# Other cuts of the last two rows, and a piece summed by two engines, in a ReLU row sum

## Chip and metric

The kernel runs on one core of a Trainium2 chip. The metric is the device time of one execution in microseconds (us); less is better. VectorE (DVE in the profile) and ScalarE (ACT) compute, SyncE (SP) issues the transfers, and 16 DMA engines carry them out.

## What is computed

The input has 32 x 512 = 16384 rows of 1024 float32 numbers, 67 MB. Each row gives one number: the sum of its positive elements.

```python
def reference(x):                     # x: (32, 512, 1024) float32
    relu_x = np.maximum(x, 0)
    return np.sum(relu_x, axis=-1).astype(np.float32)
```

## The kernel before

The rows are spread over 128 partitions, 128 rows on each. They fall into three regions of 1, 111 and 16 rows per partition (REGIONS); in the last one a partition holds 16 rows that lie one behind another in memory. The input comes in seven chunks of 16 rows per partition (CHUNKS), into a buffer `buf` with room for three chunks, and then in a tail of 8, 4 and 2 rows (TAIL) and the last two rows, which are cut into pieces. All transfers are issued by SyncE on one queue, in the order in which they are written.

In the first six chunks ScalarE applies ReLU to several rows at once (L145), and VectorE adds up each row (L160, `tensor_reduce`). In the seventh chunk and in the tail, both engines do whole rows by turns, ReLU and sum in one instruction. `on_act` (L127) does it on ScalarE and `on_dve` (L130) on VectorE; each shows in the profile as two rows, the pass itself and a short read of its accumulator.

The change is in what follows. `flat` is the place of the last two rows in `buf`, 2048 columns in one line: columns 0 to 1023 are the one row, from D = 1024 on the other. The queue brings, in this order:

| transfer | columns in `flat` | count | semaphore |
|---|---|---|---|
| first (L112) | 0 to 911 (CUT = 912) | 912 | `s_in[-3]` |
| second (L112) | 1536 to 2047 | 512 | `s_in[-2]` |
| third (L112) | 1280 to 1535 (from HEAD = 256 on) | 256 | `s_in[-1]` |
| seam (L115) | 912 to 1279, into the tile `seam` | 368 | `s_seam`, 16 counts |

The seam spans the end of the one row (w = 112 columns) and the head of the other (256). In the tile `seam` it lies between accumulators: two columns ahead of it for the two halves of the first piece, two behind it for the second and the third piece. When everything is there, one pass of ScalarE over `seam[:, 0:k]` (k = 2 + w) adds the rest of the one row to its two partial sums, and one pass of VectorE over the remaining columns does so for the other row. The partial sums are of positive numbers, so ReLU leaves them as they are.

Before these closing sums, ScalarE does the left half of the first piece and then the second piece alone (L194, L195); VectorE does the right half of the first piece and then the third (L197, L198). Both closing sums wait for `s_seam` to reach 16 + 2: the seam's transfer, the second piece and the third (L199, L202). ScalarE also waits for the halves (`s_half`).

On SyncE, the store of the first region's results is issued early. The store of the middle region (L123) waits for the third piece's transfer, and the last store (L207) for both closing sums (`s_last`). The program ends when all stores have landed.

Of the kernel before, what the change touches and what calls it, by code (L numbers as in the profile page):

```python
# [3 lines left out]
P = 128  # L4
D = 1024
# [4 lines left out]
ACT_STEPS = [[16], [7, 9], [7, 9], [7, 9], [4, 5, 7], [3, 4, 5]]  # L10
DVE_STEPS = [[4, 5, 7], [7, 4, 5], [7, 4, 5], [7, 4, 5], [4, 5, 7], [3, 4, 5]]
TAIL = [8, 4, 2]
CUT = 912
HEAD = 256


def bass_relu_sum_kernel(
# [14 lines left out]
    fp32 = mybir.dt.float32  # L32
# [5 lines left out]
    J = B * S // P  # L38
# [11 lines left out]

    buf = nc.alloc_sbuf_tensor("buf", [P, NB, BIG, D], fp32)
    w = D - CUT
    seam = nc.alloc_sbuf_tensor("seam", [P, 2 + w + HEAD + 2], fp32)
    res = nc.alloc_sbuf_tensor("res", [P, J], fp32)
    turned = nc.alloc_sbuf_tensor("turned", [P, 32], fp32)

# [1 line left out]
    s_in = [nc.alloc_semaphore(f"s_in{i}") for i in range(n_in)]  # L58
# [5 lines left out]
    s_seam = nc.alloc_semaphore("s_seam")  # L64
    s_last = nc.alloc_semaphore("s_last")
# [4 lines left out]
    sp, act, dve = nc.sync, nc.scalar, nc.vector  # L70
# [36 lines left out]

    rows = xv[-1].rearrange("p j d -> p (j d)")[:, r * D : (r + 2) * D]
    flat = buf[:, tb, r : r + 2, :].rearrange("p j d -> p (j d)")
    first, second, third = [(0, CUT), (D + D // 2, 2 * D), (D + HEAD, D + D // 2)]  # L110
    for k, (lo, hi) in enumerate((first, second, third)):
        sp.dma_start(out=flat[:, lo:hi], in_=rows[:, lo:hi]).then_inc(  # L112
            s_in[NBIG + len(TAIL) + k], 16
        )
    sp.dma_start(out=seam[:, 2 : 2 + w + HEAD], in_=rows[:, CUT : D + HEAD]).then_inc(s_seam, 16)  # L115
    sp.wait_ge(s_turn, 1)
# [9 lines left out]
    def on_act(t, acc):  # L126
        return act.activation(t, t, AF.Relu, accum_out=acc)  # L127

    def on_dve(t, acc):
        return dve.tensor_scalar(  # L130
            out=t, in0=t, scalar1=0.0, scalar2=None, op0=ALU.max, op1=ALU.add, accum_out=acc
        )
# [4 lines left out]
    k = 0  # L137
# [49 lines left out]
    lo, hi = first  # L187
    act.wait_ge(s_in[-3], 16)
    dve.wait_ge(s_in[-3], 16)
    on_act(flat[:, lo : CUT // 2], seam[:, 0:1]).then_inc(s_half, 1)  # L190
    on_dve(flat[:, CUT // 2 : hi], seam[:, 1:2]).then_inc(s_half, 1)
    k = 2 + w
    lo, hi = second
    act.wait_ge(s_in[-2], 16)  # L194
    on_act(flat[:, lo:hi], seam[:, k + HEAD : k + HEAD + 1]).then_inc(s_seam, 1)  # L195
    lo, hi = third
    dve.wait_ge(s_in[-1], 16)  # L197
    on_dve(flat[:, lo:hi], seam[:, k + HEAD + 1 : k + HEAD + 2]).then_inc(s_seam, 1)  # L198
    act.wait_ge(s_seam, 16 + 2)  # L199
    act.wait_ge(s_half, 2)  # L200
    on_act(seam[:, 0:k], res[:, J - 2 : J - 1]).then_inc(s_last, 1)
    dve.wait_ge(s_seam, 16 + 2)  # L202
    on_dve(seam[:, k : k + HEAD + 2], res[:, J - 1 : J]).then_inc(s_last, 1)


    sp.wait_ge(s_last, 2)
# [31 lines left out]
```

## Time and profile before

| what | value |
|---|---|
| time, median of 3 runs | 160.80 us (160.78 to 161.15) |
| span of the profiled execution, first to last instruction | 159.4 us |
| last semaphore record of the profiled execution | 160.85 us |
| VectorE busy | 120.6 us (76%) |
| ScalarE busy | 101.5 us (64%) |
| input read | 67.11 MB, 421 GB/s over the span |
| VectorE `tensor_reduce` of rows (L160) | 99.4 us in 18 instructions |
| ScalarE ReLU of several rows (L145) | 80.4 us in 13 instructions |

Times in the profile count from the first instruction of the span. The span leaves out what lies around it; the profiled execution's last record is at 160.85 us, so 1.46 us lie behind the span. A row such as "157.01 0.42 DVE L130" gives the start, the length, the engine and the line of an instruction; in brackets stands how long the engine had been idle ahead of it, and what ended that. L127 and L130 are the lines of the two helpers, so different passes are told apart by their shape: 128x456 is 128 partitions with 456 columns each.

### The profile page before, as it was taken

The page shows a single profiled execution, that of the slowest core. Times are in us where ns is not written, and L with a number is a line of the kernel's source. Part 1 is how long each engine was busy: PE and PEld are TensorE (multiplying, and loading weights), DVE is VectorE, ACT ScalarE, POOL GpSimd, SP SyncE. Part 2 cuts the span into 40 slices and gives each one's busy share as a digit, 9 for nine tenths or more (in the row PEclk, how much of TensorE's full clock was granted, in tenths as well). Part 3 has the DMA queues.
Part 4 walks back from the last instruction along what each step waited for, and adds up shares of the span by engine and source line. Part 5 has one row for each costly group of instructions (what it writes and reads, how often), then busy time and mean ns, then how long its engine had stood idle before and what let it go on. Part 6 is the DMA issues. An engine that isn't in the chain of part 4 may idle for free.

```text
span 159.4 us, 150 instructions
## 1 busy us (share of the span) xinstructions
DVE 120.6 (76%) x59; ACT 101.5 (64%) x54; POOL 0.2 (0%) x4
## 2 busy tenths in 40 slices
DVE  0000000009999999999999999999999999898995
ACT  3000059980799708996099941999329980496975
POOL 0000000000000000000000000000000000000000
DMA  9997996996996997989979969969969979798994
GB/s 378 493 401 339 493 526 263 526 526 263 526 493 296 526 444 345 526 378 411 526 312 477 526 263 526 526 263 526 526 263 526 444 345 526 321 469 374 417 400 142
DMA packets 2457, 67.18 MB, mean 421 GB/s; under 512 B 536, under 2 KB 792, under 8 KB 1176
## 3 DMA queue, kind: packets, MB, share of 16 engines
q1 hardware_dynamic: 2456, 67.18, 98.1%
q14 instruction: 1, 0.01, 0.0%
HBM read 67.11 MB, written 0.07 MB: 421 GB/s over the span
## 4 chain that ended last, share of the span: by engine, by line
DVE 55%; DMA 34%; ACT 9%; SPq 2%; issue 0%
DVE res L160 54%; DMA buf<-in_x_dram 34%; ACT buf L145 9%; SPq L101 1%; SPq L112 1%; DVE buf L130 0%; DVE seam L130 0%; SPq L91 0%; DVE turned L169 0%
## 5 line engine op out<-in xcount | busy, mean ns | idle before, releaser
L160 DVE TENSOR_REDUCE res<-buf 128x4 f32<-128x4096 f32 (+3 forms) x18 | 99.4, 5596 | 35.5 <-ACT buf L145 35.5
L145 ACT ACTIVATE buf<-buf 128x7168 f32<-128x7168 f32 (+5 forms) x13 | 80.4, 6233 | 46.1 <-DMA buf<-in_x_dram 46.1
L127 ACT ACTIVATE buf<-buf 128x1024 f32<-128x1024 f32 (+2 forms) x19 | 19.0, 999 | 8.9 <-DMA buf<-in_x_dram 8.9
L130 DVE TENSOR_SCALAR_CACHE_REDUCE buf<-buf 128x1024 f32<-128x1024 f32 (+2 forms) x19 | 20.7, 1143 | 1.7 <-DMA buf<-in_x_dram 1.6
L127 ACT ACTIVATION_READ_ACCUMULATOR buf<-buf 128x1 f32 x19 | 3.6, 188 | 0.0
L145 ACT ACT_TABLE_LOAD x1 | 1.3, 1283 | 1.3 <-PEq L223 1.3
L130 DVE DVE_READ_ACCUMULATOR buf<-buf 128x1 f32 x19 | 1.6, 84 | 0.0
L130 DVE TENSOR_SCALAR_CACHE_REDUCE seam<-seam 128x258 f32<-128x258 f32 x1 | 0.4, 421 | 0.0
L127 ACT ACTIVATE seam<-seam 128x114 f32<-128x114 f32 x1 | 0.3, 300 | 0.1
L169 DVE STREAM_TRANSPOSE turned<-res 128x32 f32<-128x32 f32 x1 | 0.2, 211 | 0.0
L127 ACT ACTIVATION_READ_ACCUMULATOR seam<-seam 128x1 f32 x1 | 0.2, 186 | 0.0
L223 POOL MEMSET const-bfloat16-1.0<- 128x1 bf16 x1 | 0.1, 101 | 0.0
L223 POOL MEMSET const-uint8-127<- 128x1 uint8 x1 | 0.1, 101 | 0.0
L223 POOL MEMSET const-float32-0.0<- 128x1 f32 x1 | 0.1, 98 | 0.2 <-issue 0.2
L223 POOL MEMSET const-float32-1.0<- 128x1 f32 x1 | 0.1, 98 | 0.0
L130 DVE DVE_READ_ACCUMULATOR seam<-seam 128x1 f32 x1 | 0.1, 82 | 0.0
## 6 DMA issues: line engine op xcount, KB each, us to landing
buf<-in_x_dram SPq DMA_DIRECT2D x1, 7680.0 KB, 21.1
buf<-in_x_dram SPq DMA_DIRECT2D x1, 4096.0 KB, 25.3
buf<-in_x_dram SPq DMA_DIRECT2D x1, 2048.0 KB, 29.9
buf<-in_x_dram SPq DMA_DIRECT2D x1, 1024.0 KB, 31.9
buf<-in_x_dram SPq DMA_DIRECT2D x1, 512.0 KB, 3.3
buf<-in_x_dram SPq DMA_DIRECT2D x1, 456.0 KB, 32.5
buf<-in_x_dram SPq DMA_DIRECT2D x1, 256.0 KB, 32.7
seam<-in_x_dram SPq DMA_DIRECT2D x1, 184.0 KB, 32.6
```

The source lines that it names most:

```text
L101: sp.dma_start(out=buf[:, tb, r : r + n, :], in_=xv[-1][:, r : r + n, :]).then_inc(s_in[NBIG + i], 16)
L112: sp.dma_start(out=flat[:, lo:hi], in_=rows[:, lo:hi]).then_inc(s_in[NBIG + len(TAIL) + k], 16)
L127: return act.activation(t, t, AF.Relu, accum_out=acc)
L130: return dve.tensor_scalar(out=t, in0=t, scalar1=0.0, scalar2=None, op0=ALU.max, op1=ALU.add, accum_out=acc)
L145: act.activation(t, t, AF.Relu).then_inc(s_act, 1)
L160: dve.tensor_reduce(out=res[:, c * BIG + r : c * BIG + r + n], in_=buf[:, c % NB, r : r + n, :], axis=X, op=ALU.add,).then_inc(s_dve, 1)
L169: dve.transpose(out=turned[:, :], in_=res[:, 0:32]).then_inc(s_turn, 1)
L223: nc = _bacc.Bacc("TRN2", target_bir_lowering=False, num_devices=1)
```

## The change

Four constants give the cuts. The first piece has 928 columns, the second 624, the third 192 and the seam 304 (96 of the one row, 208 of the other). The order on the queue stays. The second piece is summed by both engines: the first 420 columns (SHARE) by ScalarE, the other 204 by VectorE, which does so ahead of the third piece. So VectorE waits for the second piece's transfer too, there are three accumulators behind the seam and not two, and the closing sums wait for 16 + 3 counts.

```diff
-CUT = 912
-HEAD = 256
+CUT = 928
+HEAD = 208
+MID = 400
+SHARE = 420
...
-    seam = nc.alloc_sbuf_tensor("seam", [P, 2 + w + HEAD + 2], fp32)
+    seam = nc.alloc_sbuf_tensor("seam", [P, 2 + w + HEAD + 3], fp32)
...
-    first, second, third = [(0, CUT), (D + D // 2, 2 * D), (D + HEAD, D + D // 2)]
+    first, second, third = [(0, CUT), (D + MID, 2 * D), (D + HEAD, D + MID)]
...
     lo, hi = second
     act.wait_ge(s_in[-2], 16)
-    on_act(flat[:, lo:hi], seam[:, k + HEAD : k + HEAD + 1]).then_inc(s_seam, 1)
+    on_act(flat[:, lo : lo + SHARE], seam[:, k + HEAD : k + HEAD + 1]).then_inc(s_seam, 1)
+    dve.wait_ge(s_in[-2], 16)
+    on_dve(flat[:, lo + SHARE : hi], seam[:, k + HEAD + 1 : k + HEAD + 2]).then_inc(s_seam, 1)
     lo, hi = third
     dve.wait_ge(s_in[-1], 16)
-    on_dve(flat[:, lo:hi], seam[:, k + HEAD + 1 : k + HEAD + 2]).then_inc(s_seam, 1)
-    act.wait_ge(s_seam, 16 + 2)
+    on_dve(flat[:, lo:hi], seam[:, k + HEAD + 2 : k + HEAD + 3]).then_inc(s_seam, 1)
+    act.wait_ge(s_seam, 16 + 3)
     act.wait_ge(s_half, 2)
     on_act(seam[:, 0:k], res[:, J - 2 : J - 1]).then_inc(s_last, 1)
-    dve.wait_ge(s_seam, 16 + 2)
-    on_dve(seam[:, k : k + HEAD + 2], res[:, J - 1 : J]).then_inc(s_last, 1)
+    dve.wait_ge(s_seam, 16 + 3)
+    on_dve(seam[:, k : k + HEAD + 3], res[:, J - 1 : J]).then_inc(s_last, 1)
```

## The prediction

> **What bounds the kernel now.** I read the page first, then the chain of waits from its end backwards, then the instructions of the last 3.5 us in order of time, then the groups with shapes kept apart, for prices. The edit touches nothing that is issued ahead of the last two rows of a partition (DMA issues from 123.39 us on), so only the end can move.
>
> ```profile
> span 159.4 us, 150 instructions
> ...
> q14 instruction: 1, 0.01, 0.0%
> ```
>
> ```profile
> 124.39 32.60 DMA buf<-in_x_dram
> 156.99 0.02 issue
> 157.01 0.44 DVE buf L130 x2
> 157.45 0.02 issue
> 157.47 0.43 DVE seam L130 x2
> ```
>
> The second fence is the end of the chain: start, length, what. The third piece lands at 156.99, VectorE sums it for 0.44, and then the closing sum of the seam tile takes 0.43. In the order of time:
>
> ```profile
> 155.96 0.58 ACT L127 ACTIVATE buf<-buf 128x456 f32<-128x456 f32 x1
> 155.98 0.62 DVE L130 TENSOR_SCALAR_CACHE_REDUCE buf<-buf 128x456 f32<-128x456 f32 x1
> 156.53 0.08 DVE L130 DVE_READ_ACCUMULATOR buf<-buf 128x1 f32 x1
> 156.65 0.63 ACT L127 ACTIVATE buf<-buf 128x512 f32<-128x512 f32 x1
> 157.01 0.42 DVE L130 TENSOR_SCALAR_CACHE_REDUCE buf<-buf 128x256 f32<-128x256 f32 x1 [0.40 <-DMA buf<-in_x_dram]
> ...
> 157.47 0.30 ACT L127 ACTIVATE seam<-seam 128x114 f32<-128x114 f32 x1
> 157.47 0.42 DVE L130 TENSOR_SCALAR_CACHE_REDUCE seam<-seam 128x258 f32<-128x258 f32 x1
> 157.68 0.19 ACT L127 ACTIVATION_READ_ACCUMULATOR seam<-seam 128x1 f32 x1
> 157.82 0.08 DVE L130 DVE_READ_ACCUMULATOR seam<-seam 128x1 f32 x1
> 157.93 0.34 SPq L207 DMA_DIRECT2D out_dram<-res  x1
> ```
>
> VectorE stands idle for 0.40 us ahead of the third piece, while ScalarE works on the second: that is the room the edit uses. The trace's semaphore records give landings closer than the fences: first piece 155.934, second 156.626, third 156.988, seam 157.438. The closing sums wait for three things: ScalarE's second piece (signalled 157.380), the seam's landing (157.438) and VectorE's third piece (157.451). The chain names the last, but the landing is only 13 ns ahead of it. So taking work off the engines alone buys 13 ns; what is to gain further lies in the transfers and in the closing sums themselves.
>
> ```profile
> L130 DVE TENSOR_SCALAR_CACHE_REDUCE buf<-buf 128x1024 f32<-128x1024 f32 x17 | 19.8, 1217 | 1.3 <-DMA buf<-in_x_dram 1.2
> ...
> L127 ACT ACTIVATE buf<-buf 128x512 f32<-128x512 f32 x1 | 0.6, 630 | 0.0
> L130 DVE TENSOR_SCALAR_CACHE_REDUCE buf<-buf 128x456 f32<-128x456 f32 x1 | 0.6, 624 | 0.0
> L127 ACT ACTIVATE buf<-buf 128x456 f32<-128x456 f32 x1 | 0.6, 584 | 0.0
> ```
>
> Prices from here (mean ns of one): a VectorE sum costs (1217 - 624) / 568 = 1.04 ns a column, a ScalarE sum (630 - 584) / 56 = 0.82 ns. Packets of the DMA records: 2048 bytes 84 ns, 1024 bytes 46 ns, so 0.037 ns a byte, and with 8 packets of a piece on each of the 16 engines 1.19 ns a column of a piece.
>
> **The change, part by part.**
>
> *Transfers.* The order on the queue and the total of 2048 columns stay, so the seam's landing stays at 157.438 by bytes alone. The first piece has 16 columns more (+19 ns: 155.953). After the second, 1552 columns are in instead of 1424 (+152 ns: 156.778). After the third, 1744 instead of 1680 (+76 ns: 157.064).
>
> *Where the pieces begin.* The second and the third now begin 5696 and 4928 bytes into the two rows, no longer at a multiple of 256 bytes. Before, only the seam does so (3648), and its 1472-byte packets take 66 ns in the median where the line through 1024 and 2048 bytes gives 62.6; so I price an odd start at 3.4 ns a packet, 27 ns a piece: second 156.805, third 157.118, seam 157.492. The bounds: nothing at all below; above, the slowest of those packets took 82 ns, 19 ns more than the line, 0.16 us a piece, 0.31 us for both.
>
> The Trainium skill speaks against this part (DMA: Bandwidth & Descriptors, "How a descriptor splits into AXI transactions"): a read that does not begin at a 256-byte boundary starts at the boundary below and pays for the unused bytes, in beats of 32. By that rule the two pieces would fetch 2 beats more per packet each and the seam, now 128 bytes above a boundary and not 64, 2 more as well; 6 beats times 8 packets at that page's 850 MHz would make an estimate of 0.06 us, where the row above makes 0.05. The trace's 66 against 62.6 ns agrees with it in sign. No sum below uses it.
>
> *The first piece's halves* grow from 456 to 464 columns: +8 ns on VectorE, +7 ns on ScalarE. ScalarE is done at 156.66 and VectorE at 156.62, both ahead of the second landing at 156.805, which hides it. Without that cover it would cost 8 ns.
>
> *The second piece* is split. Both engines start 0.024 us after it lands (156.988 to 157.012 in the third): 156.829. ScalarE's 512 columns took 0.732 us to their signal; 420 take 92 x 0.82 = 0.075 less: 157.486, later than the 157.380 of before, as the piece lands later. VectorE's new sum is 204 columns: 420 - 52 x 1.04 = 366 ns. The wait is one more in front of the third piece's sum, and behind it stand the third sum and VectorE's closing sum. Sums in a row start their own length less 73 ns apart (154.838 to 155.982 for 1217 ns, with a wait between), so VectorE is free for the third at 157.122. That lies in the idle 0.40 us. Its own transfer releases the third later, at 157.118 + 0.024 = 157.142: the new sum is hidden, by 20 ns. If that cover were gone, each ns would go onto the end.
>
> *The third piece* has 192 columns: 0.439 - 64 x 1.04 ns = 0.372 us to its signal, so 157.514. That is the last of the three, with the seam at 157.492. The closing sums start 23 ns later, 157.537, against 157.474: +0.063.
>
> *The closing sums.* VectorE's has 211 columns in place of 258: 0.429 - 0.049 = 0.380. ScalarE's has 98 in place of 114: 0.391 - 0.013 = 0.378. So -0.049, and the two are level: a shorter VectorE part would bring nothing more.
>
> *The stores.* SyncE's store of the middle results (L123) waits for the third piece, so goes 0.13 later. It landed at 159.047, the last store at 159.349: 0.30 of cover. The issue at 157.21 ends 0.34 later, ahead of 157.9, when SyncE is wanted for the last store. Cost nothing; with the cover gone, what exceeds 0.30.
>
> *The sum*: +0.063 - 0.049 = +0.014 us. With no price for the odd starts: VectorE's third sum starts at 157.095, ends 157.467, the closing sums start at 157.490: +0.016 - 0.049 = -0.033. With the dear price the third lands at 157.376, is summed at 157.772, and the sum is 0.321 - 0.049 = +0.27. Between these the median row is the nearest, as it prices what most packets pay. The profiled execution has a span of 159.39 and its last semaphore records at 160.85; the runs' median is 160.80, so it is an ordinary one. Forecast: 160.85 + 0.01 for such an execution, **160.8** on the scale of the median. What an edit gives here is a few hundredths of a microsecond; what a measurement can tell from no change is 0.3%, 0.48 us.
>
> **The rivals.**
>
> *VectorE becomes the bound.* The sum added ahead of the third piece could lose its overlap (73 ns) and its slack (20 ns), and the odd starts be dear (+0.27). For it: three sums stand in a row with no slack worth the name. Against it: the same pair of instructions, with a wait, overlaps at 155.98. It would give 160.9 to 161.15, still no difference to be told. 10%.
>
> *Slower: code fetched at the end.* The one packet of the instruction queue (first fence) is 8192 bytes, starts at 159.21 and takes 0.49 us, after the sums and ahead of the last records at 160.85. VectorE's stream gets one sum longer, which shows as two rows. If that moves it over the edge at which another such block is fetched, and the engine stands still for it once the third piece is there or past the span, the price is 0.49 us or, with the wait for it, twice that: 161.3 to 161.8. It decides from the moment the fetch starts later than the engine needs it. For it: an edge is evidently near for some engine. Against it: the trace does not tell whose; such a fetch in the middle of the idle 30 us from 125 on would cost nothing. 12%.
>
> The Trainium skill (Runtime: NRT & Kernel Launch, "Instruction fetch mechanics") holds crossing such an edge to be mostly hidden, in blocks of 16 KiB; here the packet is 8 KiB, and the rule would make this rival's price near nothing.
>
> *Faster: the landings draw together.* The 16 engines deliver their shares of one piece 0.46 us apart (seam: 156.98 to 157.44). Were smaller, differently cut last pieces to even that out, the seam would be there at about 157.0, the closing sums would start 0.42 earlier and be 0.05 shorter: 160.33. Against it: the same spread stands at the large chunks (117.83 to 118.34), so it comes with the stream and not with the cuts. 7%.
>
> **How the numbers follow.** The forecast has 71%, with 160.65 to 161.1 as its own range (the sum's lower end on the fastest run, 160.78, with a tenth for the draw; the upper with half of the dear price and the same tenth); VectorE as the bound 10%; both are "no difference": 81%. Slower has 12%, faster 7%. For eight in ten the range is 160.4 to 161.3: it takes in both priced ends around runs that lay between 160.78 and 161.15, the lower part of the fetch and not quite the even landings.
>
> **What would show it.** Second landing near 156.81, third near 157.12, seam near 157.49; a VectorE sum of 204 columns at 156.83 of 0.37 us and no idle worth naming ahead of the third; closing sums at 157.54, level on both engines; the last store issued at about 157.95. Packets of 2496 and 768 bytes at 104 and 40 ns would settle the odd starts (101 and 37 on the line). I am wrong if the last store is issued more than 0.3 us from 157.93, or if a stretch ahead of 155.9 or behind 159.4 has changed: then it is something that this view does not hold.

## The result and the profile after

The changed kernel takes 161.48 us (median of 5 runs, 161.39 to 161.67) against 160.78 for the kernel before (160.77 to 161.15): ratio 1.0042, interval 1.0032 to 1.0053. It is 0.7 us slower, where no difference was forecast, with a range that ended at 161.3. Its profiled execution has a span of 160.3 us and its last semaphore record at 161.77, so 1.46 us lie behind the span as before. What was lost lies inside it. The profiled execution is the slowest of the five (161.67), so its trace loses a little more than the medians do. Of the page, the lines that were shown of before:

```profile
span 160.3 us, 152 instructions
...
q14 instruction: 1, 0.01, 0.0%
```

There are two rows more, the added sum and its accumulator's read, and still one code packet. That it moved does not show on the page.

The end of the chain of waits (start, length, what) reads so after the change:

```profile
123.96 33.77 DMA buf<-in_x_dram
157.72 0.02 issue
157.75 0.66 DVE buf L132 x4
158.40 0.02 issue
158.43 0.38 DVE seam L132 x2
```

The order is as forecast: VectorE sums its share of the second piece and then the third without a gap (0.66 us for both), and the closing sum is 0.05 us shorter than before. But the second piece lands at 157.72 in place of the 156.81 that was forecast. The instructions in order of time show where that begins:

```profile
150.95 1.21 DVE L132 TENSOR_SCALAR_CACHE_REDUCE buf<-buf 128x1024 f32<-128x1024 f32 x1
...
153.29 1.06 ACT L129 ACTIVATE buf<-buf 128x1024 f32<-128x1024 f32 x1 [1.50 <-DMA buf<-in_x_dram]
153.29 1.22 DVE L132 TENSOR_SCALAR_CACHE_REDUCE buf<-buf 128x1024 f32<-128x1024 f32 x1 [1.12 <-DMA buf<-in_x_dram]
...
155.72 1.06 ACT L129 ACTIVATE buf<-buf 128x1024 f32<-128x1024 f32 x1 [0.25 <-DMA buf<-in_x_dram]
...
156.91 0.59 ACT L129 ACTIVATE buf<-buf 128x464 f32<-128x464 f32 x1
156.91 0.64 DVE L132 TENSOR_SCALAR_CACHE_REDUCE buf<-buf 128x464 f32<-128x464 f32 x1
157.75 0.55 ACT L129 ACTIVATE buf<-buf 128x420 f32<-128x420 f32 x1 [0.15 <-DMA buf<-in_x_dram]
157.75 0.37 DVE L132 TENSOR_SCALAR_CACHE_REDUCE buf<-buf 128x204 f32<-128x204 f32 x1 [0.19 <-DMA buf<-in_x_dram]
```

Both engines already wait for the four rows of the tail, until 153.29. In the kernel before that was 152.32:

```profile
152.32 1.06 ACT L127 ACTIVATE buf<-buf 128x1024 f32<-128x1024 f32 x1 [0.62 <-DMA buf<-in_x_dram]
152.32 1.22 DVE L130 TENSOR_SCALAR_CACHE_REDUCE buf<-buf 128x1024 f32<-128x1024 f32 x1 [0.24 <-DMA buf<-in_x_dram]
```

No transfer in front of this point was edited. Each transfer's semaphore gets 16 counts, read here as one from each of the 16 DMA engines; of the four rows' counts, 15 are in by 152.392, and the last comes at 153.264, 0.87 us later. Before, the last two were 0.02 apart (152.280 and 152.301). So one DMA engine is late, and it stays so: in the seam's landing the last count is 0.79 behind the next.

What it did in between is in the DMA queues. Of the kernel before, the stretch from 159.0 to 159.39 us, behind the sums; of the changed kernel, the stretch from 151.5 to 152.5 (the columns are packets, MB and the share of 16 engines' time):

```profile
q14 instruction: 1, 0.01, 7.9%
```

```profile
q1 hardware_dynamic: 56, 0.33, 81.9%
q14 instruction: 1, 0.01, 1.9%
```

This is the one code packet of 8192 bytes of which the prediction spoke. It started at 159.21 when nothing else was under way; now it starts at 151.84, among the loads. The records do not name the engine, but by their times one chain of packets follows the code packet without a gap: the code packet from 151.84, 309 ns; then one of 4 bytes, 9 ns; then a data packet of 8192 bytes from 152.16 that takes 898 ns, where such packets take 309 in the median; then 315, 318 and 309. So this engine lost 0.309 + 0.589 = 0.90 us.

Why the packet moved is the question of the experiments. VectorE's compiled program has 4032 bytes before, 63 instructions of 64 bytes, and 4160 after, 65 instructions: the added sum counts twice, as in the profile's rows. The other engines' programs have the lengths they had.

### The profile page after: what moved, and what is told of

Same layout as the page of the kernel before. It is cut to its first block, busy times and chain, and to the rows that moved or that the text cites. A ratio compares the mean times of both kernels' runs of the same rounds, so it can differ in the third digit from the quotient of the medians.

```text
span 160.3 us, 152 instructions
## 1 busy us (share of the span) xinstructions
DVE 120.9 (75%) x61; ACT 101.5 (63%) x54; POOL 0.2 (0%) x4
## 4 chain that ended last, share of the span: by engine, by line
DVE 55%; DMA 34%; ACT 9%; SPq 1%; issue 0%
DVE res L162 54%; DMA buf<-in_x_dram 34%; ACT buf L147 9%; SPq L103 1%; DVE buf L132 0%; SPq L114 0%; SPq L93 0%; DVE seam L132 0%; DVE turned L171 0%
## 5 line engine op out<-in xcount | busy, mean ns | idle before, releaser
L132 DVE TENSOR_SCALAR_CACHE_REDUCE buf<-buf 128x1024 f32<-128x1024 f32 (+3 forms) x20 | 21.0, 1100 | 2.3 <-DMA buf<-in_x_dram 2.3
```

The source lines that it names most:

```text
L132: return dve.tensor_scalar(out=t, in0=t, scalar1=0.0, scalar2=None, op0=ALU.max, op1=ALU.add, accum_out=acc)
```

## The experiments

The theory: with more than 4096 bytes of VectorE code, the packet is asked for while the loads run. The rivals: the odd beginnings of the pieces, or the added sum with its wait. All times are medians; ratios are against the kernel before, timed beside them on the same chip (160.82 to 160.91).

**The cuts without the added sum.**

```diff
-    on_act(flat[:, lo : lo + SHARE], ...).then_inc(s_seam, 1)
-    dve.wait_ge(s_in[-2], 16)
-    on_dve(flat[:, lo + SHARE : hi], ...).then_inc(s_seam, 1)
+    on_act(flat[:, lo:hi], ...).then_inc(s_seam, 1)
...
-    act.wait_ge(s_seam, 16 + 3)
+    act.wait_ge(s_seam, 16 + 2)
```

> The new cuts, but ScalarE alone sums the second piece (624 columns): VectorE's program is as long as before. Theory (code fetch): VectorE's stream, two instructions longer in the changed kernel, asks for its next 8 KB of code at 151.8 us in place of 159.2, and the one DMA engine that brings it delivers all later pieces 0.9 us late. Then here the fetch is again at about 159.2, the second piece lands at about 156.8 on all engines, ScalarE's sum of it takes 0.09 us more than 512 columns did, the closing sums start at about 157.7, and the time is about 161.0 (160.9 to 161.1). Rival (the cuts: pieces that begin at odd places are slow): the landings stay at 157.7 to 158.3 as in the changed kernel, and with the longer ScalarE sum the time is 161.6 or more. Rival (the added VectorE sum costs it): the same 161.0 as the theory, but then the next run, which keeps that sum, stays at 161.5.

160.98, ratio 1.0006 (0.9997 to 1.0015). The packet is at 159.52, the pieces land at 156.91, 157.20 and 157.55, ScalarE's sum of 624 columns takes 722 ns against 630, and the closing sums start at 157.78. So the cuts do not make the transfers late. This does not yet part the theory from the added sum.

**The changed kernel with a shorter VectorE program.** The sum, its wait and the cuts stay.

```diff
-DVE_STEPS = [[4, 5, 7], [7, 4, 5], [7, 4, 5], [7, 4, 5], [4, 5, 7], [3, 4, 5]]
+DVE_STEPS = [[16], [7, 4, 5], [7, 4, 5], [7, 4, 5], [4, 5, 7], [3, 4, 5]]
```

> The changed kernel as it is, but VectorE reduces the first chunk's 16 rows in one instruction, not in three, so that its program has the length it had before the change. Theory (code fetch): the fetch goes back to about 159.2, the landings to about 156.8, 157.1 and 157.5, the closing sums start at about 157.54 and the time is 160.75 to 160.85. Rivals (odd beginnings of the pieces, or the added sum with its wait): the end stays as in the changed kernel, 161.4 to 161.6.

160.82, ratio 0.9996 (0.9988 to 1.0005), against 1.0042 for the changed kernel. The end of its chain, and the code packet in the stretch from 159.0 to 159.44:

```profile
123.80 33.07 DMA buf<-in_x_dram
156.87 0.02 issue
156.89 0.66 DVE buf L132 x4
157.55 0.02 issue
157.57 0.38 DVE seam L132 x2
```

```profile
q14 instruction: 1, 0.01, 11.1%
```

The same five links as in the changed kernel; the transfer's starts 0.16 us earlier, the four behind it 0.85 to 0.86 us earlier. Both rivals fall: the cuts, the added sum and its wait are all in here.

**The same reduction merged in the kernel before**, as a control (the same one-line diff).

> The kernel before with the first chunk's 16 rows reduced by VectorE in one instruction, not three: a control for the same edit in the changed kernel. Theory (code fetch): VectorE's program is shorter still, the packet stays behind the sums at about 159.2, and the time is 160.8, no difference. Rival (the merged reduction itself gained what came back): 160.2 or less, the same 0.6 to 0.7 us below the kernel before.

161.08, ratio 1.0010 (1.0002 to 1.0019). The merging gains nothing of itself. The 0.1% that it costs does not lie in the loads: the span stays at 159.4 to 159.8 us, but 8 of the 12 executions have 1.5 to 1.7 us behind it, where every other run here has 1.3 to 1.4. Why is open. No code packet shows in the profiled execution, in the span or shortly behind it, where the expectation had one at about 159.2; VectorE's program has 61 instructions here.

**The kernel before with a longer VectorE program**, once by two instructions and once by one, in a stretch where VectorE has nothing to do.

```diff
+    spare = nc.alloc_sbuf_tensor("spare", [P, 2], fp32)
...
+    for i in range(2):
+        dve.memset(spare[:, i : i + 1], 0.0)
```

> The kernel before, with two VectorE memsets of one column of a spare tile ahead of everything, where VectorE is idle for 35 us: its program gets as long as the changed kernel's, and nothing else differs. Theory (code fetch): the 8 KB packet moves into the stream of loads, one engine's landings come some 0.9 us late, and the time is 161.4 to 161.7. Rivals (odd beginnings, added sum): no difference, 160.8, and the packet stays at 159.2.

> The kernel before with one such memset: 64 instructions of VectorE, between the 63 of before and the 65 of the changed kernel. Theory (code fetch) with an edge behind the 64th instruction (4096 bytes): 160.8 and the packet at 159.2. Theory with the edge elsewhere, or one that moves by an instruction at a time: the packet lies between 151.8 and 159.2, and the time above 161 if that is ahead of 156. Rivals: 160.8 whatever the packet does.

With two: 161.61, ratio 1.0039 (1.0025 to 1.0053). With one: 160.88, ratio 1.0002 (0.9993 to 1.0011). Of the first, the chain's end and the code packet in the stretch from 152.1 to 152.6:

```profile
158.21 0.02 issue
158.23 0.45 DVE buf L131 x2
158.68 0.02 issue
158.71 0.43 DVE seam L131 x2
```

```profile
q14 instruction: 1, 0.01, 3.9%
```

Two memsets that nobody reads make the kernel before as slow as the changed one, with the third piece landing at 158.21 in place of 156.99. Not all of these 1.22 us are the packet's: the profiled execution is the slowest of its five (161.97), and a landing ahead of the packet was 0.48 late already (147.89 against 147.41). The third piece's last count comes 0.77 behind the next. The packet starts at 152.22, and the data packet behind it takes 905 ns. With one memset, 64 instructions, the packet is at 159.42. This shows the cause without any part of the change.

**The edge from the other side**: the changed kernel with `[9, 7]` for the first chunk, 64 instructions.

> The changed kernel with the first chunk's rows reduced by VectorE in two instructions (9 and 7 rows), not three: 64 instructions of VectorE, one less than the changed kernel. Theory (an edge behind the 64th, the code packet moves into the loads beyond it): the packet at about 159.3 and 160.75 to 160.9, so one instruction is worth 0.6 us. If the place moved gradually with the length: the packet near 153 and 161.4 to 161.6.

160.81, ratio 0.9995 (0.9986 to 1.0004), the packet at 159.18. The step lies between the 64th and the 65th instruction, in both kernels.

**Still longer programs**: the kernel before with 10 and with 34 memsets.

> The kernel before with ten one-column memsets of VectorE at its start, 73 instructions in place of 63 (two of them gave 65). Theory A (the packet is asked for when VectorE comes to a certain instruction of its stream): the packet moves some eight instructions, four row sums or 4 to 5 us, ahead of the 152.2 of the run with two, to about 147, and the end is as late as there, 161.4 to 161.7, since an engine once late stays late in a stream without gaps. Theory B (the place depends only on the edge being passed): the packet stays at about 152, same time.

> The same with 34 memsets, 97 instructions. Theory A: the packet moves ahead by the 32 instructions since the run with two, out of the row sums and in among the large reductions, to somewhere between 40 and 125 us, and the time is again 161.4 to 161.7 if the lateness of one engine stays to the end; 160.8 to 161.0 if the stream makes up for it on the way. Theory B: the packet at about 152, 161.4 to 161.7.

161.49, ratio 1.0040 (1.0027 to 1.0053), and 161.42, ratio 1.0033 (1.0020 to 1.0046). The packet starts at 142.02 and at 91.04. Of the second, the packet in the stretch from 90 to 92 us, and the chain's end:

```profile
q1 hardware_dynamic: 16, 1.05, 122.9%
q14 instruction: 1, 0.01, 1.0%
```

```profile
124.48 33.15 DMA buf<-in_x_dram
157.63 0.02 issue
157.65 0.45 DVE buf L131 x2
158.10 0.02 issue
158.12 0.43 DVE seam L131 x2
```

A packet 66 us ahead of the last pieces' landings costs nearly what one 6 us ahead does: the last of the 16 counts comes 0.61 us behind the next in the chunk that lands at 99.68, and 0.57 in the seam at 158.10. So the late engine made up 0.04 us in 58 us; the data queue took 97.7% of the 16 engines' span in this run, which leaves it little room. Theory A is right in its direction, the packet moves ahead with the program's length, but its size was off: eight more instructions moved it by 10.2 us and not by 4 to 5. Counted in the profile's VectorE rows (the page's count and two rows of VectorE's sequencer), the packet starts after 48 of 63 rows in the changed kernel, after 50 of 63, 42 of 71 and 47 of 95 in those with 2, 10 and 34 memsets, and after the last row wherever the program has 63 or 64 instructions. So it is not asked for at one fixed row; what sets the place is open.

**A longer ScalarE program.**

```diff
-ACT_STEPS = [[16], [7, 9], [7, 9], [7, 9], [4, 5, 7], [3, 4, 5]]
+ACT_STEPS = [[3, 3, 3, 3, 2, 1, 1], [7, 9], [7, 9], [7, 9], [4, 5, 7], [3, 4, 5]]
```

> The kernel before with ScalarE's first chunk in seven passes (3, 3, 3, 3, 2, 1, 1 rows) in place of one of 16 rows: ScalarE's program has 65 instructions in place of 59, VectorE's stays at 63. The extra passes cost some 0.6 us of ScalarE at 22 to 36 us, where VectorE can start earlier for them. Theory, if the edge holds for every engine's program: an 8 KB packet comes in the middle of the loads, one engine is 0.9 us late and the time is 161.4 to 161.7. Theory, if the edge is VectorE's own: 160.7 to 160.9 and the packet at 159.2.

160.86, ratio 1.0001 (0.9991 to 1.0010). Neither expectation is quite met. The stretch from 157.6 to 159.5 us holds two code packets where the others have one, at 157.88 and 159.37:

```profile
q14 instruction: 2, 0.02, 4.3%
```

The later one comes where the kernel before has its one packet (159.21), so the earlier one is taken for ScalarE's. A longer ScalarE program then brings a packet too, but at 65 instructions it starts while ScalarE's last row runs (157.82 to 158.01), behind the last load, which landed at 157.58. Where ScalarE's edge for a packet among the loads lies was not tried.

**The added sum without the cuts**, with the merged reduction, so that VectorE's program has 63 instructions.

```diff
-CUT = 928
-HEAD = 208
-MID = 400
-SHARE = 420
+CUT = 912
+HEAD = 256
+MID = 512
+SHARE = 340
```

> The second piece on both engines (340 columns on ScalarE, 172 on VectorE) with the cuts as before the change (912, 512, 256, 368), and the first chunk reduced in one instruction, so that VectorE's program keeps its 63. Theory: ScalarE is done with its share by 157.25 and VectorE is free ahead of the third piece, but the third piece and the seam land when they did, so the closing sums start at most 0.01 us earlier than in the kernel before: 160.8, no difference. Rival (ScalarE's sum of the second piece set the end): 0.1 us or more faster.

160.85, ratio 0.9999 (0.9990 to 1.0008). The closing sums start at 157.52, 0.02 behind the seam's landing at 157.50. Taking work off ScalarE alone brings nothing, as the 13 ns of the prediction said.

## Why the prediction was wrong

**The step that failed** is the prediction's first: "The edit touches nothing that is issued ahead of the last two rows of a partition (DMA issues from 123.39 us on), so only the end can move." One transfer is not issued by the kernel's lines: VectorE's code. The added sum made that program longer than 4096 bytes, which moved its 8 KB packet from 159.2 to 151.8 us and made the last count of every landing from there on 0.79 to 0.88 us late. The prediction's own signs of being wrong both came: the last store is issued at 158.84, 0.91 us from 157.93, and the stretch ahead of 155.9 has changed.

**The rival that came nearest** was the slower one, "code fetched at the end". It had the packet, the added sum as its cause and the edge. It had the wrong direction and the wrong victim: the packet came earlier, not later, and VectorE never stood still for it, but one of the 16 DMA engines lost 0.90 us, and each landing waits for the last of the 16. Its sentence against itself, that "such a fetch in the middle of the idle 30 us from 125 on would cost nothing", is the error in small: SyncE's issue queue is idle there, the DMA engines are not. The page of the kernel before had said so: its data queue took 98.1% of the 16 engines' span.

```profile
q1 hardware_dynamic: 2456, 67.18, 98.1%
```

The rival's price of 161.3 to 161.8 holds the 161.48 by coincidence, since its 0.49 us was the length of a code packet with no other transfer under way, and not the loss of an engine among the loads. A chance of 12% was too little for the one named mechanism with a step in it.

**The forecast's own terms** held, once the packet is back. In the changed kernel with the shorter VectorE program, counted from the landing of the two rows ahead of the pieces (154.814 before and in the forecast, 154.858 here):

| event, us after the two rows' landing | before | forecast | measured |
|---|---|---|---|
| second piece landed | 1.812 | 1.991 | 2.007 |
| third piece landed | 2.174 | 2.304 | 2.279 |
| seam landed | 2.624 | 2.678 | 2.639 |
| closing sums start | 2.660 | 2.723 | 2.711 |
| last store issued | 3.118 | 3.132 | 3.121 |

So nothing gained and nothing lost: what the shorter closing sums give, the later landing of the second and third piece takes, and that kernel is no faster than the one before.

**The price of an odd beginning** was a misreading. Packets of 2496, 768 and 1216 bytes take 100, 36 and 53 ns in the median in the changed kernel; the line through 1024 and 2048 bytes gives 101, 37 and 53. The 66 ns of the seam's packets before was not due to where they begin: in the seven other runs with the same cuts the median is 62 in three and 66.5 to 68 in four, and the shortest take 62 in all of them, where the line gives 62.6. The Trainium skill's rule on this (DMA: Bandwidth & Descriptors, "How a descriptor splits into AXI transactions") is not seen in these packets' times. The landings do not settle it: by bytes alone the forecast of the table would have been 1.964, 2.250 and 2.624, so they come 0.02 to 0.04 us later than that, but with the cuts of before and no packet among the loads the second piece's landing alone lies between 1.81 and 1.85 from run to run.

**The Trainium skill on code** (Runtime: NRT & Kernel Launch, "Instruction fetch mechanics") calls the crossing of a block's edge mostly hidden. For VectorE that is so here: each of its waits from 140 us on is for data. For the kernel it is not: 0.6 to 0.8 us in the four runs with the packet among the loads. Why, another page says (DMA: Bandwidth & Descriptors, "Queues, rings and completion order"): the queue that refills code runs on the same 16 engines as the data and takes turns with it, packet by packet. The packet of 151.84, between two data packets of one engine, agrees with it.

**The rivals "VectorE becomes the bound" and "the landings draw together"** did not occur. The third sum followed the added one with no gap, with an overlap of 76 ns where the prediction took 73; and with the new cuts and the shorter program the 16 counts of the seam's landing lie 0.42 us apart (157.08 to 157.50), against 0.46 before.

## What to carry to other kernels

Where a stream of loads keeps all DMA engines full to the end, count VectorE's instructions ahead of an edit, and look for the code packet in the DMA queues of both profiles: one instruction too many can put 8 KB of code among the loads. The price is paid once, on one DMA engine, and what exceeds that engine's lead over the last one reaches the end, since every landing waits for the last engine. An instruction saved elsewhere in that program, here in the first chunk's reduction some 100 us ahead, took it back. The edge behind the 64th instruction is that of this program; no run here tells whether other programs have it at the same place.

## What was not expected of the hardware

The code packet itself takes 309 ns among the loads, as long as a data packet of its size. The data packet behind it on the same engine takes longer by about twice that, whatever its size: 898 ns for 309 with 8192 bytes, 905 for 309, 1772 for 1213 with 32768 bytes, and 3036 for 2418 with 65536, so 0.56 to 0.62 us more. Why is open; no run here tells. The landings' loss differs, 0.88 us at most in the changed kernel and about 0.6 in those with 10 and 34 memsets; that it depends on how far ahead of the last the affected engine was is an inference, as the records do not name the engine. Matched by their times they agree: when the packet came, the affected engine was 0.16 and 0.13 us ahead of the last in the changed kernel and with two memsets, and 0.37 and 0.42 with 10 and 34.
